# Attention value products: two rounded halves of V at full width, or plain float32 in two column halves

## The chip, the cores and the metric

One core of a Trainium2 chip runs the whole layer. The metric is the device time of one execution in microseconds (us). The kernel before takes 1442.31 us, the median of 3 runs (1439.19 to 1443.56).

## The reference, cut to what matters

The layer has two causal token mixers on the same 1024 tokens. NSA has eight heads in two groups, each with a compressed branch, a branch of selected blocks and a sliding window; DSA has eight heads over a latent. Both end in the same step: probabilities times values.

```python
# NSA, for a block of 128 tokens
o_cmp = jnp.einsum('ghtc,cgd->tghd', p_cmp, v_cmp)
o_slc = jnp.einsum('ghtk,gtkd->tghd', p, v_g)
o_win = jnp.einsum('ghtk,kgd->tghd', p, vw)
o = gates[..., 0:1] * o_cmp + gates[..., 1:2] * o_slc + gates[..., 2:3] * o_win
# DSA (heads, latent, values; shapes cut)
o_lat = jnp.einsum('htk,tkr->thr', p, c_g)
o_b = jnp.einsum('bthr,hrd->bthd', o_lat, w_uv)
```

A mixture of experts follows. All inputs are float32.

## The kernel before, in words

**The whole.** Most products on PE have operands of the type `F32R`, a rounded float32. The helper `split` makes two of them from one float32 operand: ACT casts the high part (line 59), DVE subtracts it from the source to get the low part (line 60), and products of high and low parts add up in PSUM. The stages are: projections (line 204) with the indexer of DSA and a search for its top keys on DVE (line 324), the attention of the 16 heads in the order of `ORDER`, the merge of the branches (line 711), the output projection and routing (line 978), and the experts (lines 1086 and 1109). Instructions are put in order on each engine by a planner that simulates the program; only the experts' order on PE is written out by hand.

**A head.** A head works on its 8 blocks of 128 queries in two halves of four (`gq`). Per query block, PE writes scores to a PSUM tile `s` (NSA: lines 573 and 574, compressed keys lines 580 and 581; DSA: lines 651 and 652, and 654 adds the selection mask). `softmax_part` adds the bias on DVE with a running extreme (line 482) and takes the exponential with its sum on ACT (line 484) into a tile `pb` or `pw`. POOL scales the rows by the reciprocal sums (`scale_rows`, line 465). Since all of the 16 blocks of 64 keys can be selected, the selected branch of NSA is causal attention over all keys.

**The value products.** The probabilities have queries on the partitions; the product needs keys there. `values` gets a list of runs: one key block with up to four query blocks that see it. It packs the runs into banks of at most four blocks (512 columns). Per bank, `transposed_pair` transposes up to four blocks on PE into a PSUM tile `pt` (line 490, three buffers) and splits it: ACT writes `pth`, DVE writes `ptl` (lines 59 and 60). Then PE takes, per run, a product with `pth` (line 545) and one with `ptl` (line 546). The stationary operand is a value block of 128 columns: the 64 columns of V's high part beside the 64 of its low part (`vv`, `vcc`, made at lines 163 and 164 and 420 and 421; `vb` for DSA, made by `dsa_values` at lines 626 and 627 from the products of line 622). So the output tile `pv` (one buffer) has the products with V's high part on partitions 0 to 63 and with its low part on 64 to 127, and `finish` adds the two halves, either through DRAM and POOL (line 514) or directly (lines 519 and 520).

**How many.** Over all heads there are 240 banks: 200 of 512 columns and 40 of 256.

Of the kernel before, what the change touches and what calls it, by code (L numbers as in the profile page):

```python
# [44 lines left out]
def layer_kernel(ctx: ExitStack, tc: tile.TileContext, A, out, dbg=None):  # L45
# [63 lines left out]
    ats = ExitStack()  # L109
    att = ats.enter_context(tc.tile_pool(name="att", bufs=1, side="right"))  # L110
    u0 = ctx.enter_context(tc.tile_pool(name="u0", bufs=1))
    vv = u0.tile([P, NT, 4, P], F32R, name="vv", tag="slot7")
    kch = att.tile([P, 2, 64], F32R, name="kch")
    kcl = att.tile([P, 2, 64], F32R, name="kcl")
    vcc = att.tile([P, 2, P], F32R, name="vcc")
    G.memset(f(vcc[0:64]), 0.0)
    cks = ExitStack()
    ckn = cks.enter_context(tc.tile_pool(name="ckp", bufs=1)).tile([P, NT, P], F32, name="ckn")
    cth = att.tile([P, T], F32R, name="cth")
# [17 lines left out]
    with tc.tile_pool(name="cr", bufs=1, side="right") as cr, tc.tile_pool(name="cr2", bufs=2, side="right") as cr2:  # L137
        big = [ps.tile([P, T], F32, name="s") for _ in range(3)]
        acc = [b[:, c] for b in big for c in HALF] + [ps.tile([P, 512], F32, name=n) for n in ("pt", "pv")]
        for k in range(KD):  # L140
            xw = cr2.tile([P, T + WN], F32, name="xw", bufs=4)
            nc.sync.dma_start(xw, A["xw"][k])
            xr, wr = xw[:, 0:T], xw[:, T:T + WN]
            split(xh[:, k], xl[:, k], xr)
            wh = cr2.tile([P, WN], F32R, name="wnh")
            wl = cr2.tile([P, WN], F32R, name="wnl")
            split(wh, wl, wr)
            for i in range(NT):
                ts = slice(i * P, (i + 1) * P)
                o = acc[i][:, :WN]  # L150
                PE.matmul(o, xh[:, k, ts], wh, start=(k == 0), stop=False)
                PE.matmul(o, xh[:, k, ts], wl, start=False, stop=False)
                PE.matmul(o, xl[:, k, ts], wh, start=False, stop=(k == KD - 1))
        nc.sync.dma_start(ident, A["ident"])
        V.tensor_copy(ident_b, ident)
        sq = cr.tile([P, NT], F32, name="sq")
        rstd = cr.tile([P, NT], F32, name="rstd")
        junk = cr.tile([P, P], F32, name="junk")
        gck = cr.tile([P, P], F32, name="gck")
        nc.sync.dma_start(gck, A["ckv_g"].partition_broadcast(P))  # L160
        for i in range(NT):
            src = acc[i][:, 0:256].rearrange("p (a d) -> p a d", a=4)
            S.copy(vv[:, i, :, 0:64], src)
            V.tensor_tensor(vv[:, i, :, 64:128], src, f(vv[:, i, :, 0:64]), op=ALU.subtract)
            S.activation(junk, acc[i][:, 280:408], AF.Square, accum_out=sq[:, i:i + 1])
            V.tensor_copy(ckn[:, i], acc[i][:, 280:408])
            V.tensor_copy(sig[:, i], acc[i][:, 256:280])
            V.tensor_scalar(wi[:, i], acc[i][:, 408:412], 0.5, None, op0=ALU.mult)  # L168
        V.tensor_scalar(sq, sq, 1.0 / 128, 1e-6, op0=ALU.mult, op1=ALU.add)
        G.tensor_tensor(rstd, sq, mhalf, op=ALU.pow)  # L170
        for i in range(NT):
            V.scalar_tensor_tensor(ckn[:, i], ckn[:, i], rstd[:, i:i + 1], gck, op0=ALU.mult, op1=ALU.mult)
# [212 lines left out]
    def compress(n, cp):  # L385
# [30 lines left out]
        if n == "kc":  # L416
            split(flat(kch), flat(kcl), t[:, 0:P])
        else:
            for g in range(2):
                S.copy(vcc[64:128, g, 0:64], t[g * 64:g * 64 + 64, 0:64])  # L420
                V.tensor_tensor(vcc[64:128, g, 64:128], t[g * 64:g * 64 + 64, 0:64], f(vcc[64:128, g, 0:64]),
                                op=ALU.subtract)

    with tc.tile_pool(name="cp", bufs=1, side="right") as cp, tc.tile_pool(name="bt", bufs=1, side="right") as bt:
        bias = bias_tables(bt)
# [64 lines left out]
            PE.transpose(t[:rows, x * P:(x + 1) * P], c, ident)  # L490
        return t[:rows, :n]

    def transposed_pair(cols, rows=P):
        t = transposed(cols, rows)
        n = P * len(cols)
        h = aw1.tile([P, 512], F32R, name="pth", bufs=3)
        l = aw1.tile([P, 512], F32R, name="ptl", bufs=3)
        split(h[:rows, :n], l[:rows, :n], t)
        return h[:rows, :n], l[:rows, :n]

    mc = aw0.tile([P, 8, 120], F32, name="mc")
    nc.sync.dma_start(mc, bass.AP(bc_d.tensor, bc_d.offset + 7, [[WP, P], [P * WP, 8], [1, 120]]))
# [21 lines left out]
            nc.sync.dma_start(od[n][h // 2][:, HALF[gq]], t)  # L524

    pair = {}

    def values(o, todo, gq, first, last):

        banks = []  # L530
        for run in sorted(todo, key=lambda r: -len(r[1])):
            for b in banks:
                if sum(len(r[1]) for r in b) + len(run[1]) <= 4:
                    b.append(run)
                    break
            else:
                banks.append([run])
        assert len(banks[0][0][1]) == 4
        for y, b in enumerate(banks):
            ph, pl = transposed_pair([c for r in b for c in r[1]])  # L540
            x = 0
            for z, (v, cols, i0) in enumerate(b):
                oo = o[:, (i0 - 4 * gq) * P:(i0 - 4 * gq + len(cols)) * P]
                n = slice(x, x + len(cols) * P)
                PE.matmul(oo, v, ph[:, n], start=first and y == 0, stop=False)  # L545
                PE.matmul(oo, v, pl[:, n], start=False, stop=last and y == len(banks) - 1 and z == len(b) - 1)  # L546
                x += len(cols) * P

    def nsa_head(h, kv, fin):
        g = h // 4  # L550
# [7 lines left out]
        for gq in range(2):  # L558
# [3 lines left out]
            for part in range(2):  # L562
                st = aw1.tile([P, 2, 8], F32, name="st", bufs=3)
                PR, PC, PS = {}, {}, {}
                for i in I4:
                    ts = slice(i * P, (i + 1) * P)
                    k0 = 0 if part == 0 else max(0, i - 4)
                    n = P * (i + 1 - k0)
                    kh, kl = (ksh, ksl) if part == 0 else (kwh, kwl)
                    s = ps.tile([P, T], F32, name="s")  # L570
                    for c in range(0, n, 512):
                        e = min(n, c + 512)
                        PE.matmul(s[:, c:e], q[:, ts], kh[:, k0 * P + c:k0 * P + e], start=True, stop=False)  # L573
                        PE.matmul(s[:, c:e], q[:, ts], kl[:, k0 * P + c:k0 * P + e], start=False, stop=True)  # L574
                    j = i % 4
                    if part == 0:
                        PR[i] = aw1.tile([P, T], F32, name="pb", bufs=8)[:, :n]
                        softmax_part(s[:, :n], m[:, T - n:T], PR[i], st, j)
                    else:
                        PE.matmul(s[:, 640:704], q[:, ts], kch[:, g], start=True, stop=False)  # L580
                        PE.matmul(s[:, 640:704], q[:, ts], kcl[:, g], start=False, stop=True)
                        pb = pwp.tile([P, 704], F32, name="pw", bufs=6)
                        PR[i], PC[i], PS[i] = pb[:, :n], pb[:, n:n + 64], pb[:, n - 64:n + 64]
                        softmax_part(s[:, :n], mw[:, 640 - n:640], PR[i], st, j)
                        softmax_part(s[:, 640:704], mc[:, h, 56 - 8 * i:120 - 8 * i], PC[i], st, 4 + j)
# [4 lines left out]
                if part:  # L590
                    V.tensor_tensor(st[:, 1, 4:8], st[:, 1, 4:8], sig[:, 4 * gq:4 * gq + 4, 3 * h], op=ALU.mult)
                for i in I4:
                    scale_rows(PR[i], st[:, 1, i % 4:i % 4 + 1])
                    if part:
                        scale_rows(PC[i], st[:, 1, 4 + i % 4:5 + i % 4])
                for k in range(4 * gq + 4):
                    ii = [i for i in I4 if i >= k and (part == 0 or i - 4 <= k)]
                    k0 = [0 if part == 0 else max(0, i - 4) for i in range(NT)]
                    todo.append((vv[:, k, 2 * part + g],
                                 [PR[i][:, (k - k0[i]) * P:(k - k0[i] + 1) * P] for i in ii], ii[0]))  # L600
# [17 lines left out]
    def dsa_values(h):  # L618
        s = ps.tile([P, T], F32, name="s")
        for i in range(NT):  # L620
            for c, w in ((cth, uvh), (cth, uvl), (ctl, uvh)):
                PE.matmul(s[:, i * P:(i + 1) * P], c[:, i * P:(i + 1) * P], w[:, h * 64:h * 64 + P],
                          start=(c is cth and w is uvh), stop=(c is ctl))
        vb = aw2.tile([P, NT, 2, P], F32R, name="vb", bufs=1)
        sv = s.rearrange("p (i j d) -> p i j d", i=NT, j=2)
        S.copy(vb[:, :, :, 0:64], sv)
        V.tensor_tensor(vb[:, :, :, 64:128], sv, f(vb[:, :, :, 0:64]), op=ALU.subtract)
        return vb

    def dsa_head(h, vb, fin):  # L630
# [10 lines left out]
        for gq in range(2):  # L641
# [3 lines left out]
            for i in I4:  # L645
# [3 lines left out]
                for c in range(0, n, 512):  # L649
# [2 lines left out]
                    PE.matmul(s[:, c:e], q[:, ts], kl[:, c:e], start=False, stop=i < 2)  # L652
                    if i >= 2:
                        PE.matmul(s[:, c:e], ident_b, selm[:, OFF[i] + c:OFF[i] + e], start=False, stop=True)
                PR[i] = aw1.tile([P, T], F32, name="pb", bufs=8)[:, :n]
                softmax_part(s[:, :n], m[:, T - n:T], PR[i], st, i % 4)
            V.tensor_scalar(st[:, 1], st[:, 1], 1e-30, None, op0=ALU.max)
            V.reciprocal(st[:, 1], st[:, 1])  # L658
            for i in I4:
                x = st[:, 1, i % 4:i % 4 + 1]  # L660
                if (i % 2 and h >= 6):
                    V.tensor_scalar(PR[i], PR[i], x, None, op0=ALU.mult)
                else:
                    scale_rows(PR[i], x)
            o = ps.tile([P, 512], F32, name="pv")
            todo = []
            for k in range(4 * gq + 4):
                ii = [i for i in I4 if i >= k]
                todo.append((vb[:, k, h % 2], [PR[i][:, k * P:(k + 1) * P] for i in ii], ii[0]))
            values(o, todo, gq, True, True)  # L670
            finish("b", h, gq, o, fin)
# [128 lines left out]

    RING = [5, 6, 7, 7, 17, 9, 10, 11, 12, 13, 14, 15, 16, 1, 2, 0]
    weights, loads = [], []
    sync = mybir.DependencyInfo(mybir.DependencyClass.Sync, mybir.DependencyReason.DATA)

    def prefetch(n=1):
        for _ in range(min(n, 3 * NE - len(weights))):
# [505 lines left out]
```

## Time and profile before

| what | value |
|---|---|
| timed runs | 1439.19, 1442.31, 1443.56 us |
| the profiled execution | 1442.7 us, its span 1440.9 us |
| PE busy | 1330.8 us, 92% of the span |
| PE weight loads busy | 1099.4 us, 76% |
| DVE busy | 1120.3 us, 78% |
| ACT busy | 764.8 us, 53% |
| POOL busy | 457.6 us, 32% |
| mean granted TensorE clock | 0.966 of full |

The page's busy time of PE counts each matmul up to a modelled end, and matmuls overlap in the pipeline, so a busy PE is not PE at its peak. Columns of the lists of groups: line, engine, operation, output tile and input tiles, partitions by elements and type, count, busy time in us and mean in ns, then the engine's idle time just before them and what ended it. PEld is the loading of weights.

### The profile page before, as it was taken

Reading aid. Unit: us, or ns where it says so; the run is one execution under the profiler, and the core shown is the slowest. Engines: PE = TensorE matmul, PEld = TensorE weight load, DVE = VectorE, ACT = ScalarE, POOL = GpSimd, SP = SyncE. Lnnn points to the kernel's source line nnn. Section 1 sums busy time; section 2 is a strip of 40 time slices with the busy share of each in tenths; the row PEclk is TensorE's granted clock in tenths of the full one; section 3 lists DMA queues with packets and bytes.
Section 4 is the critical chain, followed back from the end, with each engine's and each line's share of the span. In section 5 each row is a group of like instructions: output and inputs, shape, how many; then the busy total and the mean of one; then the engine's idle time right before and its main releaser. Section 6 shows DMA issues by size and latency. Waiting matters only on the chain.

```text
span 1440.9 us, 20097 instructions
## 1 busy us (share of the span) xinstructions
PE 1330.8 (92%) x6795; PEld 1099.4 (76%) x6795; DVE 1120.3 (78%) x2276; ACT 764.8 (53%) x1388; POOL 457.6 (32%) x457
## 2 busy tenths in 40 slices
PE   8999999999999999989999999999869999998950
PEld 8878888888887878878788778888757877776730
DVE  4323699889997878788889956654869999998946
ACT  4323323322117887778789732300248888877734
POOL 1112323312213344454444200002344444443315
PEclk9999999999998999999999999999979999999975
DMA  6023333497423332823521334765659999999834
GB/s 226 15 80 132 112 133 141 156 279 263 154 89 116 96 85 73 220 77 93 147 66 38 123 148 163 289 222 195 237 194 337 348 330 316 318 336 331 289 96 192
DMA packets 69476, 261.36 MB, mean 181 GB/s; under 512 B 15091, under 2 KB 16973, under 8 KB 57084
## 3 DMA queue, kind: packets, MB, share of 16 engines
q1 hardware_dynamic: 59644, 243.24, 48.9%
q0 software_dynamic: 9728, 16.82, 5.0%
q8 instruction: 54, 0.88, 0.3%
q14 instruction: 50, 0.41, 0.1%
HBM read 219.19 MB, written 70.70 MB: 201 GB/s over the span
## 4 chain that ended last, share of the span: by engine, by line
PE 60%; issue 16%; POOL 12%; DVE 5%; ACT 4%; DMA 2%; POOLq 0%; SPq 0%; DVEq 0%; ACTq 0%
PE s L204 24%; PE s L711 6%; PE s L978 6%; PE pt L490 5%; POOL acc_d L1114 5%; PE pv L546 3%; PE pv L545 3%; POOL xg L1046 2%; POOL xg L1043 2%; PE s L573 2%; PE pv L393 1%; PE s L574 1%; ACT pw L484 1%; PE s L652 1%; PE s L651 1%
## 5 line engine op out<-in xcount | busy, mean ns | idle before, releaser
L1086 PE MATMUL pt<-slot,slot 128*128 128x512 f32 x768 | 198.8, 405 | 11.9 <-DVE slot L1074 5.5
L1074 DVE TENSOR_TENSOR slot<-slot,slot 128x1024 fp32r<-128x1024 f32 x158 | 189.0, 1221 | 16.0 <-ACT slot L1073 10.0
L1073 ACT CAST slot<-slot 128x1024 fp32r<-128x1024 f32 x158 | 163.8, 1049 | 37.0 <-PE pt L1086 24.6
L1086 PEld LDWEIGHTS pt<-slot,slot 128*128 128x128 f32 x768 | 141.1, 190 | 51.6 <-DVE slot L1074 10.0
L186 POOL TENSOR_TENSOR wl<-wr,wh 128x1024 fp32r<-128x1024 f32 x39 | 95.0, 2438 | 262.0 <-ACT wh L185 262.0
L324 DVE TENSOR_SCALAR_CACHE_REDUCE jk<-idx,cand 128x384 bf16<-128x384 f32 (+1 forms) x186 | 164.4, 942 | 1.2
L60 DVE TENSOR_TENSOR ptl<-pt,pth 128x512 fp32r<-128x512 f32 (+1 forms) x240 | 148.3, 639 | 20.6 <-ACT pth L59 19.6
L59 ACT CAST pth<-pt 128x512 fp32r<-128x512 f32 (+1 forms) x240 | 128.5, 549 | 52.5 <-PE pt L490 44.3
L204 PE MATMUL s<-xh,wh 128*128 128x512 f32 x496 | 154.1, 391 | 2.3 <-DVE wi L168 1.4
L204 PE MATMUL s<-xh,wl 128*128 128x512 f32 x496 | 154.0, 390 | 0.0
L204 PE MATMUL s<-xl,wh 128*128 128x512 f32 x496 | 153.6, 389 | 0.0
L465 POOL TENSOR_SCALAR pb<-pb,st 128x128 f32<-128x128 f32 (+3 forms) x120 | 92.1, 786 | 183.4 <-DVE st L658 61.0
L185 ACT CAST wh<-wr 128x1024 fp32r<-128x1024 f32 x39 | 41.0, 1051 | 190.3 <-PE s L204 86.5
L1114 POOL DMA_INDIRECT acc_d<-wr,tkv x32 | 76.2, 2382 | 138.6 <-DVE wr L1113 138.6
L204 PEld LDWEIGHTS s<-xh,wh 128*128 128x128 f32 x496 | 92.2, 188 | 22.7 <-issue 2.6
L204 PEld LDWEIGHTS s<-xl,wh 128*128 128x128 f32 x496 | 93.1, 188 | 19.3
L204 PEld LDWEIGHTS s<-xh,wl 128*128 128x128 f32 x496 | 93.0, 188 | 19.2
L484 ACT ACTIVATE pb<-pb,st 128x128 f32<-128x128 f32 (+7 forms) x128 | 99.7, 780 | 12.0 <-DVE st L482 11.2
L1109 PE MATMUL s<-slot,hT 128*128 128x512 f32 x384 | 100.8, 408 | 2.0 <-DVE hT L60 1.5
L490 PE MATMUL pt<-ident,pb 128*128 128x128 f32 x576 | 92.7, 282 | 2.0 <-POOL pb L465 1.4
L978 PE MATMUL s<-slot,slot 128*128 128x512 f32 x384 | 93.3, 398 | 0.0
L1109 PEld LDWEIGHTS s<-slot,hT 128*128 128x128 f32 x384 | 70.5, 191 | 27.0 <-DVE hT L60 9.7
(345 smaller groups left out, 2932.5 us busy)
## 6 DMA issues: line engine op xcount, KB each, us to landing
slot<-in_w_ex_dram SPq DMA_DIRECT2D x79, 1024.0 KB
wr<-in_w_tt_dram SPq DMA_DIRECT2D x31, 512.0 KB
ring<-in_w_ex_dram SPq DMA_DIRECT2D x12, 1024.0 KB
b_d<-r_d SPq DMA_DIRECT2D x16, 576.0 KB
xw<-in_xw_dram SPq DMA_DIRECT2D x8, 718.0 KB
last<-in_w_ex_dram SPq DMA_DIRECT2D x5, 1024.0 KB
z_ga<-sh SPq DMA_DIRECT2D x8, 512.0 KB
slot<-b_d SPq DMA_DIRECT2D x8, 512.0 KB
```

Source lines behind the costliest of these rows:

```text
L59: S.copy(h, src)
L60: V.tensor_tensor(l, src, f(h), op=ALU.subtract)
L204: PE.matmul(z[:, c], w[:, k * P:(k + 1) * P], xx[:, k, c], start=(k == 0 and w is wh and xx is xh), stop=(k == KD - 1 and w is wl))
L324: V.tensor_scalar(jk[:, :n], idx[:, OFF[i]:OFF[i] + n], t, None, op0=op, op1=ALU.add, accum_out=cnt[:, i - 2:i - 1])
L484: S.activation(p, p, AF.Exp, bias=st[:, 0, j:j + 1], scale=-1.0, accum_out=st[:, 1, j:j + 1])
L490: PE.transpose(t[:rows, x * P:(x + 1) * P], c, ident)
L978: mm = PE.matmul(s[:, HALF[c]], MH[i // 2][a][:, k, (i % 2) * P:(i % 2) * P + P], WO[k][:, b, HALF[c]], start=(k == 0 and x == 0), stop=(k ...
L1073: S.copy(w[:, 0], self.w[k2 // 4][:, k2 % 4 // 2])
L1074: d = V.tensor_tensor(w[:, 1], self.w[k2 // 4][:, k2 % 4 // 2], f(w[:, 0]), op=ALU.subtract).ins
L1086: PE.matmul(self.a, self.xt[:, a, k * P:(k + 1) * P], w[:, b, (k - k2) * 512:(k - k2 + 1) * 512], start=(k == 0 and x == 0), stop=(k == KD ...
L1109: PE.matmul(s[:, c], self.hT[:, a, k * P:(k + 1) * P], w[:, b, c], start=(k == 0 and x == 0), stop=(k == 1 and x == 2))
L1114: d = G.indirect_dma_start(out=acc_d, out_offset=bass.IndirectOffsetOnAxis(ap=self.tok, axis=0), in_=y, in_offset=None, bounds_check=T - 1 ...
```

## The change

V is no longer split: `vv`, `vcc` and `vb` are float32 with 64 columns. The transposed probabilities are not split either: `flipped` makes one float32 copy of a bank, on ACT or on DVE. Banks are taken in pairs, called lanes here: the first bank's products write partitions 0 to 63 of `pv`, the second's 64 to 127, so that each product uses half of the array's columns. `finish` adds the two halves as before. If the number of banks is odd, the last one is divided into two; if a pair has at most four blocks in all, one transposition and one ACT copy serve both. The first product of a pair also waits for the pair's last copy. In a head's first half, key block 1 is given a zero block of probabilities for query block 0 (`score_tile` clears it on POOL), so that the first two banks both cover all four query blocks.

```diff
-    vv = u0.tile([P, NT, 4, P], F32R, name="vv", tag="slot7")
+    vv = u0.tile([P, NT, 4, 64], F32, name="vv", tag="slot7")
...
-    vcc = att.tile([P, 2, P], F32R, name="vcc")
-    G.memset(f(vcc[0:64]), 0.0)
+    vcc = att.tile([P, 2, 64], F32, name="vcc")
+    G.memset(vcc[0:64], 0.0)
...
-            S.copy(vv[:, i, :, 0:64], src)
-            V.tensor_tensor(vv[:, i, :, 64:128], src, f(vv[:, i, :, 0:64]), op=ALU.subtract)
+            S.copy(vv[:, i], src)
...
-    def transposed_pair(cols, rows=P):
-        t = transposed(cols, rows)
+    def flipped(cols, eng):
+        t = transposed(cols)
         n = P * len(cols)
-        h = aw1.tile([P, 512], F32R, name="pth", bufs=3)
-        l = aw1.tile([P, 512], F32R, name="ptl", bufs=3)
-        split(h[:rows, :n], l[:rows, :n], t)
-        return h[:rows, :n], l[:rows, :n]
+        h = aw1.tile([P, 512], F32, name="pth", bufs=6)
+        return h[:, :n], (S.copy if eng is S else V.tensor_copy)(h[:, :n], t).ins
...
-        assert len(banks[0][0][1]) == 4
-        for y, b in enumerate(banks):
-            ph, pl = transposed_pair([c for r in b for c in r[1]])
+        assert not first or all(len(banks[x][0][1]) == 4 for x in range(2))
+        if len(banks) % 2:
+            half = (sum(len(r[1]) for r in banks[-1]) + 1) // 2
+            ends = [[], []]
+            for v, cols, i0 in banks.pop():
+                a, b = cols[:half], cols[half:]
+                half -= len(a)
+                for x, (c, i) in enumerate(((a, i0), (b, i0 + len(a)))):
+                    if c:
+                        ends[x].append((v, c, i))
+            banks += ends
+        for y in range(0, len(banks), 2):
+            lanes, copies = [], []
+            short = sum(len(r[1]) for b in banks[y:y + 2] for r in b) <= 4
+            if short:
+                h, d = flipped([c for b in banks[y:y + 2] for r in b for c in r[1]], S)
+                copies.append(d)
             x = 0
-            for z, (v, cols, i0) in enumerate(b):
-                oo = o[:, (i0 - 4 * gq) * P:(i0 - 4 * gq + len(cols)) * P]
-                n = slice(x, x + len(cols) * P)
-                PE.matmul(oo, v, ph[:, n], start=first and y == 0, stop=False)
-                PE.matmul(oo, v, pl[:, n], start=False, stop=last and y == len(banks) - 1 and z == len(b) - 1)
-                x += len(cols) * P
+            for z in range(2):
+                if not short:
+                    h, d = flipped([c for r in banks[y + z] for c in r[1]], (S, V)[z])
+                    copies.append(d)
+                    x = 0
+                lane = []
+                for v, cols, i0 in banks[y + z]:
+                    lane.append((z, v, h[:, x:x + len(cols) * P], (i0 - 4 * gq) * P))
+                    x += len(cols) * P
+                lanes.append(lane)
+            steps = [lane[x] for x in range(max(map(len, lanes))) for lane in lanes if x < len(lane)]
+            for x, (z, v, m, c) in enumerate(steps):
+                end = last and y + 2 == len(banks) and not any(q[0] == z for q in steps[x + 1:])
+                d = PE.matmul(o[z * 64:z * 64 + 64, c:c + m.shape[1]], v, m,
+                              start=first and y == 0 and x < 2, stop=end).ins
+                if x == 0:
+                    tc.add_manual_dep(d, copies[-1].name, sync, reason="both halves together")
+
+    def score_tile(i):
+        p = aw1.tile([P, T], F32, name="pb", bufs=8)
+        if i == 0:
+            G.memset(p[:, P:2 * P], 0.0)
+        return p
...
-                    ii = [i for i in I4 if i >= k and (part == 0 or i - 4 <= k)]
+                    ii = [i for i in I4 if (i >= k or (i, k, part) == (0, 1, 0)) and (part == 0 or i - 4 <= k)]
...
-        vb = aw2.tile([P, NT, 2, P], F32R, name="vb", bufs=1)
-        sv = s.rearrange("p (i j d) -> p i j d", i=NT, j=2)
-        S.copy(vb[:, :, :, 0:64], sv)
-        V.tensor_tensor(vb[:, :, :, 64:128], sv, f(vb[:, :, :, 0:64]), op=ALU.subtract)
+        vb = aw2.tile([P, NT, 2, 64], F32, name="vb", bufs=2)
+        S.copy(vb, s.rearrange("p (i j d) -> p i j d", i=NT, j=2))
...
-                ii = [i for i in I4 if i >= k]
+                ii = [i for i in I4 if i >= k or (i, k) == (0, 1)]
```

## Rows read from the trace of the kernel before

**Rows 1.** The page: span, and PE's busy tenths in 40 slices of the span

```profile
span 1440.9 us, 20097 instructions
...
PE   8999999999999999989999999999869999998950
```

**Rows 2.** Busy time by stretch: the attention, 436 to 842 us

```profile
core 0: us, PE busy (x) PEld busy (x) DVE busy (x) ACT busy (x) POOL busy (x), PEclk, DMA share, GB/s
436.00:842.00 406.00, 389.14 (x2459) 330.68 (x2459) 342.29 (x939) 324.03 (x808) 164.15 (x253) 0.98 0.36 107
```

**Rows 3.** The chain of waits from 436 to 842 us, shares by line

```profile
by line: PE pt L490 17.8%; PE pv L546 10.8%; PE pv L545 9.9%; issue 5.4%; PE s L573 5.4%; PE s L574 4.9%; ACT pw L484 4.5%; PE s L652 4.2%; PE s L651 3.8%; PE s L654 3.6%; DVE ptl L60 3.6%; DVE pb L482 3.0%; PE s L711 2.6%; ACT pth L59 2.4%
```

**Rows 4.** Waits in the attention: us in total, times, longest us

```profile
ACT pth L59 <- PE pt L490: 44.3, 62, 3.5
DVE ptl L60 <- ACT pth L59: 19.6, 43, 1.4
PEld pv L546 <- DVE ptl L60: 6.6, 8, 2.4
PE pv L546 <- DVE ptl L60: 4.5, 4, 2.1
```

**Rows 5.** Line 545: matmuls, ns min/median/max, first and last start us, forms

```profile
L545 PE MATMUL pv<-pth,vv x192: 220/369/587, 448.2 to 806.7; 128*128 128x512 f32 x72, 128*128 128x384 f32 x40, 128*128 128x128 f32 x40, 128*128 128x256 f32 x40
...
L545 PE MATMUL pv<-pth,vb x96: 220/380/628, 484.3 to 841.0; 128*128 128x512 f32 x48, 128*128 128x384 f32 x16, 128*128 128x128 f32 x16, 128*128 128x256 f32 x16
...
L545 PE MATMUL pv<-pth,vcc x16: 392/477/526, 461.6 to 801.8; 128*128 128x512 f32 x16
```

**Rows 6.** A piece of the chain; then PE in order of time: start us, us

```profile
399.98 34.77 PE s L204 x154
...
950.62 3.64 PE L978 MATMUL s<-slot,slot 128*128 128x512 f32 x15
954.09 1.87 PE L955 MATMUL pt<-wrt,hT 128*128 128x36 f32 x16
955.80 1.07 PE L490 MATMUL pt<-ident,wr 128*128 128x128 f32 x8
```

**Rows 7.** Lines 922 (plain float32) and 580 (rounded): 64 columns, ns min/median/max

```profile
L922 PEld LDWEIGHTS pv<-val,at_place x32: 188/192/338, 984.5 to 1051.0; 128*128 128x128 f32 x32
L922 PE MATMUL pv<-val,at_place x32: 218/275/474, 984.7 to 1051.1; 128*128 128x64 f32 x32
...
L580 PE MATMUL s<-kch,slot x64: 192/245/362, 438.8 to 775.4; 128*128 128x64 f32 x64
```

**Rows 8.** The same view of PE's other lines in the attention: counts and forms

```profile
L490 PE MATMUL pt<-ident,pb x576: 270/272/475, 441.4 to 838.2; 128*128 128x128 f32 x192
...
L490 PE MATMUL pt<-ident,pw x304: 270/272/330, 453.8 to 802.6; 128*128 128x128 f32 x152
...
L573 PE MATMUL s<-slot,slot x192: 218/394/775, 436.1 to 775.2; 128*128 128x512 f32 x88, 128*128 128x128 f32 x56, 128*128 128x256 f32 x24, 128*128 128x384 f32 x24
...
L651 PE MATMUL s<-kbh,q x96: 222/422/589, 463.6 to 819.4; 128*128 128x512 f32 x48, 128*128 128x128 f32 x16, 128*128 128x256 f32 x16, 128*128 128x384 f32 x16
...
L654 PE MATMUL s<-selm,ident_b x80: 230/389/393, 467.5 to 820.0; 128*128 128x512 bf16 x48, 128*128 128x384 bf16 x16, 128*128 128x128 bf16 x8, 128*128 128x256 bf16 x8
```

**Rows 9.** Groups by form, ACT and DVE in the attention

```profile
L60 DVE TENSOR_TENSOR ptl<-pt,pth 128x512 fp32r<-128x512 f32 x200 | 133.2, 684 | 20.3 <-ACT pth L59 19.4
L59 ACT CAST pth<-pt 128x512 fp32r<-128x512 f32 x200 | 114.2, 584 | 50.8 <-PE pt L490 42.8 <-PE pv L545 5.6 <-DVE ptl L60 1.6
L60 DVE TENSOR_TENSOR ptl<-pt,pth 128x256 fp32r<-128x256 f32 x40 | 16.5, 413 | 0.3 <-ACT pth L59 0.2
L59 ACT CAST pth<-pt 128x256 fp32r<-128x256 f32 x40 | 15.0, 375 | 1.7 <-PE pt L490 1.6
L507 ACT COPY fin<-pv 128x512 f32<-128x512 f32 x20 | 11.6, 582 | 2.3 <-PE pv L546 2.3
L627 DVE TENSOR_TENSOR vb<-s,vb 128x1024 fp32r<-128x1024 f32 x4 | 4.9, 1220 | 2.6 <-ACT vb L626 2.6
```

**Rows 10.** Groups by form on POOL, whole program and attention

```profile
L1043 POOL MEMSET xg<- 128x1024 f32 x30 | 28.7, 956 | 49.7 <-PE s L1063 49.7
...
L465 POOL TENSOR_SCALAR pb<-pb,st 128x640 f32<-128x640 f32 x16 | 14.4, 898 | 102.9 <-DVE st L658 39.2 <-PE pv L546 15.1 <-ACT pth L59 14.1
```

More of the change, by code (lines that the diff above doesn't have):

```diff
@@ L419, in compress @@
             for g in range(2):
-                S.copy(vcc[64:128, g, 0:64], t[g * 64:g * 64 + 64, 0:64])
-                V.tensor_tensor(vcc[64:128, g, 64:128], t[g * 64:g * 64 + 64, 0:64], f(vcc[64:128, g, 0:64]),
-                                op=ALU.subtract)
+                S.copy(vcc[64:128, g], t[g * 64:g * 64 + 64, 0:64])
     with tc.tile_pool(name="cp", bufs=1, side="right") as cp, tc.tile_pool(name="bt", bufs=1, side="right") as bt:
@@ L526, in layer_kernel @@
     pair = {}
+    sync = mybir.DependencyInfo(mybir.DependencyClass.Sync, mybir.DependencyReason.DATA)
     def values(o, todo, gq, first, last):
@@ L576, in nsa_head @@
                     if part == 0:
-                        PR[i] = aw1.tile([P, T], F32, name="pb", bufs=8)[:, :n]
-                        softmax_part(s[:, :n], m[:, T - n:T], PR[i], st, j)
+                        PR[i] = score_tile(i)
+                        softmax_part(s[:, :n], m[:, T - n:T], PR[i][:, :n], st, j)
                     else:
@@ L592, in nsa_head @@
                 for i in I4:
-                    scale_rows(PR[i], st[:, 1, i % 4:i % 4 + 1])
+                    scale_rows(PR[i][:, :P * (i + 1 - (max(0, i - 4) if part else 0))], st[:, 1, i % 4:i % 4 + 1])
                     if part:
@@ L654, in dsa_head @@
                         PE.matmul(s[:, c:e], ident_b, selm[:, OFF[i] + c:OFF[i] + e], start=False, stop=True)
-                PR[i] = aw1.tile([P, T], F32, name="pb", bufs=8)[:, :n]
-                softmax_part(s[:, :n], m[:, T - n:T], PR[i], st, i % 4)
+                PR[i] = score_tile(i)
+                softmax_part(s[:, :n], m[:, T - n:T], PR[i][:, :n], st, i % 4)
             V.tensor_scalar(st[:, 1], st[:, 1], 1e-30, None, op0=ALU.max)
@@ L659, in dsa_head @@
             for i in I4:
-                x = st[:, 1, i % 4:i % 4 + 1]
+                x, p = st[:, 1, i % 4:i % 4 + 1], PR[i][:, :P * (i + 1)]
                 if (i % 2 and h >= 6):
-                    V.tensor_scalar(PR[i], PR[i], x, None, op0=ALU.mult)
+                    V.tensor_scalar(p, p, x, None, op0=ALU.mult)
                 else:
-                    scale_rows(PR[i], x)
+                    scale_rows(p, x)
             o = ps.tile([P, 512], F32, name="pv")
@@ L802, in layer_kernel @@
     weights, loads = [], []
-    sync = mybir.DependencyInfo(mybir.DependencyClass.Sync, mybir.DependencyReason.DATA)
     def prefetch(n=1):
```

## The prediction

> **What bounds the kernel now.** First the page's slices: TensorE is busy 80 to 99% of nearly every slice [rows 1], so I ask in which stage the change lies and what paces it there. The value products run from 448 to 841 us; the stage around them, the attention, is 436 to 842 us. The table by stretch gives PE 389, DVE 342 and ACT 324 of its 406 us, at nearly the full clock [rows 2]. The chain of that stretch goes through PE for most of its length, a fifth of it in the value products and about a sixth in the transposes [rows 3]. The waits show ACT waiting for transposes, DVE for ACT's half of the split, and PE for DVE's half, 11.1 us by name [rows 4]. So PE sets the end, with DVE and ACT close behind.
>
> PE's busy time overstates its work, since ends are modelled. Starts are better: 154 products of 512 columns take 34.77 us in the chain, 226 ns each, and eight transposes follow one another at about 110 ns (1.07 us less the last one's 0.27 gives 0.80 over seven steps) [rows 6]. I price 512 columns at 226, 384 at 170, 256 at 113 and 128 at 109 ns. The value products of one line are 136, 56, 56 and 56 of these [rows 5], and the other line has as many: 2 x (30.7 + 9.5 + 6.3 + 6.1) = 105 us. The stage's other work from the counts in [rows 8]: 880 transposes 96 us, NSA scores (L573, and L574 the same) 66, DSA scores (L651, L652 the same, L654) 50, and 128 compressed scores, 91 full-length and 96 short products in the rest, 45. Together 361 us. The stage lasts 406, so 45 us of it PE waits, or starts late.
>
> **What the change removes on ACT and DVE.** Before, each of 240 banks has an ACT copy and a DVE subtraction: ACT 114.2 + 15.0, DVE 133.2 + 16.5 us [rows 9]. Afterwards each bank has one copy, on ACT or on DVE. Packing the runs as the code does, an NSA head has 9 ACT copies of 512, one of 384, one of 256, and 8 DVE copies of 512 and one of 256; a DSA head has 4, 1, 1 on ACT and 4 of 512 on DVE. Over eight heads each: ACT 104 x 0.582 (L507 is such a copy) + 16 x 0.48 (between the forms) + 16 x 0.375 = 74 us, saving 55; DVE 96 x 0.684 + 8 x 0.413 = 69, if a copy costs what the subtraction does, saving 81, and L627's 4.9 [rows 9]. DVE falls to about 256 and ACT to 269 of 406 us. Neither is the bound, so this counts only through PE's 45 us of waiting. At least the named 11.1 us [rows 4] go; at most all 45. I take the middle, 28: what is left waits on score banks and softmax, which stay. The first stage loses eight subtractions of vv; a microsecond at most, and I count none.
>
> **What it does on PE.** Plain float32 is in the trace: L922 issues 16 products and has 32 records, each with its own weight load [rows 7]. So one product is two loads and two matmuls. How long one streams: the shortest 64-column matmul is 218 ns in plain float32 (L922) against 192 in the rounded type (L580) [rows 7]; 26 ns is what 64 columns take at 226 ns per 512 (28). So each record passes its columns twice, and a product four times. That rests on modelled ends and on 64 columns; L955's records, 106 ns apart [rows 6], would hide either, since no products with weights of 128 columns start closer together here. The bounds per product of 512 are then 452 ns (one pass per record) and 904 (two); I take 904.
>
> One block of 128 columns in one record is 113 ns; call that a unit. The blocks: an NSA head has 75 (one is the added zero block), a DSA head 37. The two lanes go to the two halves of the array. What a pair of lanes costs depends on how far the halves run at once, which no row shows; the three ways are the forecast and two rivals.
>
> In the forecast the halves run side by side, but records start in program order. Lane 0's product is issued whole before lane 1's: high 0, low 0, high 1, low 1. Low 0 needs high 0 out of its own half, and high 1 stands behind low 0, so high 1 runs beside low 0 and low 1 alone at the end: a pair of full banks takes three records, 12 units, where full overlap would take 8. Between pairs stand the next transposes, since a pair's copies have to be done first, so one pair rarely starts beside the last record of another. Counted so: an NSA head's first half has pairs of 12 + 5 units (selected) and 12 + 8 (window and compressed), its second 12 + 12 + 12 + 3 and 12 + 12 + 11: 111. A DSA head: 17 + 39 = 56. Eight of each: 1336 units, 151 us. Against 105 that is +46, and the 16 added transposes of zeros are 1.7 us.
>
> The Trainium skill, "TensorE: Matmul & The Clock Gate", part 3 under "What overlaps and what doesn't", says that matmuls keep program order in start and end; by that rule the three-record pair follows. No run here shows two halves at work.
>
> Unpriced on PE: a change between full and half array, twice for each of 136 pairs. In [rows 6] three kinds of product of the full array follow each other with no gap (each group starts before the last one's modelled end), so the lower end is nothing. At most each switch exposes a product's whole latency, 192 less 28 ns [rows 7]: 272 x 0.164 = 45 us. I take nothing, the nearer row, and keep the end for the range. The Trainium skill, "TensorEngine Tiling (Array Packing)", under "Key Properties", says that switching the tiling mode drains the engine; by it the 45 us would be nearer.
>
> **The rest.** POOL writes zeros into 128 columns of a tile for 16 half-heads, at most 0.96 us each (the row is for 1024 columns), 15 us in all; POOL idles over 100 us in one of its groups alone [rows 10], which hides it. It stands in front of the row scaling in POOL's order and waits for a free buffer of eight; if that cover failed, PE's transposes would be late by up to those 15 us, mostly in the first half-heads. The new wait of a pair's first product for the second copy holds PE's in-order queue, transposes and scores behind it, up to one copy, 0.68 us, for 136 pairs 93 us at worst; but before, the low product waited for ACT and DVE in turn, 1.27 us after its transposes, and lost 11 us, so it is in the 28. The second vb buffer lets the next DSA pair start early: nothing or a gain below the 4.9 us of L627.
>
> **The sum.** Against the profiled execution, 1442.7 us (span 1440.9; the median of the timed runs is 1442.3): 1442.7 + 46 + 2 - 28 = 1463. PE's work would then be 409 us, more than the stage now lasts, so no relief elsewhere makes this case faster. Its own range, relief 45 to 11 and switches 0 to half their bound: 1446 to 1502.
>
> **Rivals.**
> - Full overlap, faster. If a record for a busy half does not hold up the other half, or pairs follow each other directly, a pair takes 8 units: 39 block lengths per NSA head and 19 per DSA head, 58 x 8 x 2 = 928 units, 105 us, just what it is now. Then PE's work is unchanged and the 28 us of waiting go: 1442.7 + 2 - 28 = 1417 (1400 with all 45). For it: DVE and ACT lose a quarter and a sixth of their time, and the stage waits 45 us. Against it: lane order in the code, and pairs isolated by transposes. It decides as soon as more than about half of the third records overlap: then +23 meets -28. The Trainium skill, "TensorEngine Tiling (Array Packing)", under "Key Properties", says too that different tiles can load weights and multiply in parallel; by that sentence this rival would be the forecast.
> - The halves do not run at once (the change does not do what it says): (75 + 37) x 8 x 2 = 1792 units, 203 us, +98: 1442.7 + 98 + 2 - 28 = 1515. For it: no row shows any overlap. PE would be busy without a gap.
> - One pass per record: 668 units in the forecast's order, 75 us, -30: 1387. Against it the 26 ns of [rows 7].
> - The planner orders the whole program by its own costs, so other waits may move; a few microseconds either way round 1443.
>
> **Chances.** Records in order 0.40; full overlap 0.32; no overlap 0.18; one pass 0.04; planner noise about an unchanged time 0.06. The range reaches from full overlap with most of the waits gone to no overlap: 1402 to 1514. A difference of 0.3%, 4.3 us, can be told from none. Faster: 0.32 + 0.04 and a little of the noise, 0.37; same 0.08; slower 0.55.
>
> **What would show it.** In the changed trace each value product must have two records of 64 columns, 640 in all. If the forecast holds, in a pair the second lane's first record starts with the first lane's second, about 450 ns after the first, and the next transpose starts about 1.36 us after the pair began; with full overlap 0.9, with none 1.8. Stage 436 to 842 should grow by about 20 us, DVE fall to about 256, ACT to 269. It is wrong if the stage shrinks, if both lanes' first records start together, or if time moves outside this stage.

## The result and the profile after

The changed kernel takes 1463.0 us (median of 4 runs, 1460.86 to 1466.08) against 1442.55: ratio 1.0144, 95% interval 1.0128 to 1.0160, or 20.4 us slower. The forecast said 1463. Yet the 46 us that it added on PE and the 28 us that it took off for waiting did not come about as forecast, and a cost that it put at nothing did. These errors cancel, so the number was met by luck; the rest of this document is about that.

The page of the kernel after, its span and PE's slices:

```profile
span 1464.3 us, 19725 instructions
...
PE   8999999999999999999999999999969999998950
```

Busy time of the attention after, which now runs from about 438 to 864 us (columns as in [rows 2]):

```profile
438.00:864.00 426.00, 408.11 (x2493) 274.80 (x2507) 274.66 (x800) 282.14 (x705) 163.98 (x268) 0.99 0.34 102
```

The stretch is 20 us longer than in [rows 2]. DVE is busy 68 us less and ACT 42 less, and the stage is longer all the same. The loss is in this stage: from the first score product to the first output projection it took 436.1 to 924.5 us before and takes 438.5 to 946.5 now, 19.6 us more. The projection's row before, and then now (first and last starts stand behind the durations):

```profile
L978 PE MATMUL s<-slot,slot x384: 387/395/482, 924.5 to 1032.6; 128*128 128x512 f32 x192
```

```profile
L1004 PE MATMUL s<-slot,slot x384: 387/396/482, 946.5 to 1054.7; 128*128 128x512 f32 x192
```

The value products of the kernel after (line 566), to be read against [rows 5]:

```profile
L566 PE MATMUL pv<-pth,vv x400: 272/486/644, 450.3 to 819.2; 128*64 128x512 f32 x54, 128*64 128x128 f32 x36, 128*64 128x256 f32 x22, 128*64 128x384 f32 x22
...
L566 PE MATMUL pv<-pth,vb x208: 272/592/932, 487.1 to 862.8; 128*64 128x512 f32 x56, 128*64 128x128 f32 x32, 128*64 128x256 f32 x8, 128*64 128x384 f32 x8
...
L566 PE MATMUL pv<-pth,vcc x32: 592/618/643, 459.0 to 816.4; 128*64 128x512 f32 x32
```

640 records of 64 columns, two for each of 320 products. PE in order of time, two pairs of lanes (start us, us, what):

```profile
561.85 0.34 PE L681 MATMUL s<-selm,ident_b 128*128 128x384 bf16 x1
562.12 0.64 PE L566 MATMUL pv<-pth,vcc 128*64 128x512 f32 x1
562.13 0.86 PE L566 MATMUL pv<-pth,vv 128*64 128x384 f32 x2
562.60 0.59 PE L566 MATMUL pv<-pth,vcc 128*64 128x512 f32 x1
562.82 0.38 PE L566 MATMUL pv<-pth,vv 128*64 128x128 f32 x2
563.13 0.66 PE L487 MATMUL pt<-ident,pb 128*128 128x128 f32 x4
...
567.28 0.28 PE L603 MATMUL s<-slot,slot 128*128 128x256 f32 x1
567.65 1.08 PE L566 MATMUL pv<-pth,vb 128*64 128x512 f32 x4
568.66 0.44 PE L602 MATMUL s<-slot,slot 128*128 128x384 f32 x1
```

In the first pair, the compressed branch's lane starts at 562.12 and the other at 562.13. Neither waits for the other's second record. The first lane's second record follows at 562.60, 0.48 us after the first: 512 columns, passed twice. The second pair, two full banks, holds PE for 1.01 us from its start to the next score product; two passes of two records side by side are 0.90, records in program order would be 1.36. So the halves run fully side by side.

But each stretch of such products (half-array products with nothing else between them) has a gap on both sides. The product before the first pair streams 384 columns, 0.17 us from 561.85, and the pair starts 0.10 us after that. The second pair starts 0.26 us after the 256 columns before it have streamed; by the 0.90 us it streams until 568.55, and the next product starts 0.11 us later. Counted over all records the trace has 119 such stretches, not 136, since some pairs follow one another directly. By the prediction's prices for streaming, the median gap is 0.09 us before a stretch and 0.11 behind it, 24 us for 119. The same count in the kernel before gives 0.004 and 0.010 us around the products of line 545.

The loader of weights shows the same (groups by form, attention, kernel after; the last column is the idle time just before them):

```profile
L487 PEld LDWEIGHTS pt<-ident,pb 128*128 128x128 f32 x592 | 65.5, 142 | 47.1 <-issue 29.1 <-POOL pb L462 11.2 <-ACT pth L494 2.6
...
L566 PEld LDWEIGHTS pv<-pth,vv 128*64 128x64 f32 x400 | 28.5, 135 | 26.7 <-issue 19.8 <-ACT pth L494 1.8 <-DVE st L479 0.9
```

The loader stood idle, waiting for nothing in the profile ("issue"), for 29.1 us before the transposes of `pb`, and 19.8 before the products with `vv`. In the kernel before it stood idle for 0.4 us on "issue" in the same group of transposes: loads ran ahead of the matmuls. Around the half-array products they don't.

```profile
L490 PEld LDWEIGHTS pt<-ident,pb 128*128 128x128 f32 x576 | 70.2, 144 | 12.2 <-POOL pb L465 2.1 <-DVE ptl L60 1.4 <-issue 0.4
```

The copies cost what was estimated:

```profile
L494 ACT COPY pth<-pt 128x512 f32<-128x512 f32 x104 | 59.4, 583 | 39.4 <-PE pt L487 38.7
...
L494 DVE COPY pth<-pt 128x512 f32<-128x512 f32 x96 | 66.0, 687 | 45.2 <-PE pt L487 44.9
```

### The profile page after: what moved, and what is told of

Its sections match the earlier page's. It is cut to its first block, busy times and chain, and to the rows that moved or that the text cites. A ratio compares the mean times of both kernels' runs of the same rounds, so it can differ in the third digit from the quotient of the medians.

```text
span 1464.3 us, 19725 instructions
## 1 busy us (share of the span) xinstructions
PE 1357.2 (93%) x6829; PEld 1050.5 (72%) x6843; DVE 1047.5 (72%) x2126; ACT 722.1 (49%) x1284; POOL 455.7 (31%) x473
## 4 chain that ended last, share of the span: by engine, by line
PE 65%; issue 16%; POOL 11%; DMA 2%; DVE 2%; ACT 2%; POOLq 0%; SPq 0%; DVEq 0%; ACTq 0%
PE s L203 23%; PE pt L487 7%; PE pv L566 7%; PE s L1004 6%; PE s L738 6%; POOL acc_d L1140 5%; POOL xg L1072 2%; PE s L602 2%; POOL xg L1069 2%; PE s L603 2%; PE pv L392 1%; PE s L678 1%; PE s L679 1%; PE pt L981 1%; PE s L681 1%
## 5 line engine op out<-in xcount | busy, mean ns | idle before, releaser
L1112 PE MATMUL pt<-slot,slot 128*128 128x512 f32 x768 | 202.6, 411 | 11.0 <-ACT slot L1099 5.6
L1112 PEld LDWEIGHTS pt<-slot,slot 128*128 128x128 f32 x768 | 144.6, 195 | 50.4 <-ACT slot L1099 7.4
L203 PEld LDWEIGHTS s<-xl,wh 128*128 128x128 f32 x496 | 94.0, 190 | 19.8
L203 PEld LDWEIGHTS s<-xh,wl 128*128 128x128 f32 x496 | 93.8, 189 | 19.6
L494 DVE COPY pth<-pt 128x512 f32<-128x512 f32 (+1 forms) x104 | 69.4, 667 | 48.7 <-PE pt L487 48.5
L487 PEld LDWEIGHTS pt<-ident,pb 128*128 128x128 f32 x592 | 65.5, 142 | 47.1 <-issue 29.1
L494 ACT COPY pth<-pt 128x512 f32<-128x512 f32 (+2 forms) x136 | 71.9, 546 | 53.4 <-PE pt L487 52.7
```

Of the source, the lines that this page charges most:

```text
L203: PE.matmul(z[:, c], w[:, k * P:(k + 1) * P], xx[:, k, c], start=(k == 0 and w is wh and xx is xh), stop=(k == KD - 1 and w is wl))
L494: return h[:, :n], (S.copy if eng is S else V.tensor_copy)(h[:, :n], t).ins
L1112: PE.matmul(self.a, self.xt[:, a, k * P:(k + 1) * P], w[:, b, (k - k2) * 512:(k - k2 + 1) * 512], start=(k == 0 and x == 0), stop=(k == KD ...
```

## The experiments

Three questions were open: what the relief of ACT and DVE was worth, what a stretch of half-array products costs beside its streaming, and whether the added wait or the products themselves were the loss.

**1. The relief by itself, in the kernel before.**

```diff
-        l = aw1.tile([P, 512], F32R, name="ptl", bufs=3)
-        split(h[:rows, :n], l[:rows, :n], t)
-        return h[:rows, :n], l[:rows, :n]
+        turn[0] += 1
+        (S.copy if turn[0] % 2 else V.tensor_copy)(h[:rows, :n], t)
+        return h[:rows, :n], h[:rows, :n]
```

(`pth` gets six buffers.)

> The kernel before, with one copy per bank, on ACT and DVE in turn, in place of cast and subtraction; both products of a run read this one copy (the low part of the probabilities is left out, the high part is counted twice). PE's instructions are those of before, so this is the relief of ACT and DVE by itself. If the relief is worth what the prediction took, 28 us of PE's 45 us of waiting: about 1414 us. If, as the trace after suggests, PE is paced by its own work and most waits stay: 1430 to 1442 us.

Measured: 1486.66 us against 1443.26 (ratio 1.0303, 1.0284 to 1.0322). The whole time can't be read here: with other values the routing differs, and line 1088 of the experts does 792 products where the kernel before does 768. So only what lies ahead of the routing counts. The first group is scores, the second output projection, the third experts:

```profile
L575 PE MATMUL s<-slot,slot x192: 218/393/775, 437.1 to 781.9; 128*128 128x512 f32 x88, 128*128 128x128 f32 x56, 128*128 128x256 f32 x24, 128*128 128x384 f32 x24
...
L980 PE MATMUL s<-slot,slot x384: 387/395/482, 929.6 to 1037.8; 128*128 128x512 f32 x192
...
L1088 PE MATMUL pt<-slot,slot x792: 388/396/795, 1065.4 to 1427.8; 128*128 128x512 f32 x198
```

From the first score to the output projection 492.5 us, where before had 488.4. The busy time says that the relief was there:

```profile
437.00:848.00 411.00, 390.17 (x2444) 331.74 (x2459) 285.53 (x820) 273.29 (x689) 162.83 (x253) 0.97 0.36 106
```

DVE 57 us and ACT 51 us less than in [rows 2], and no gain at all; the granted clock was 0.97 where it was 0.98 before. The waiting moved. The planner orders the program anew for every kernel here, and PE, which waited 4.5 us for `ptl` before [rows 4], now waits longer for POOL's scaled rows and for score banks. The kernel before, and then this one:

```profile
PE s L573 <- DVE st L482: 1.9, 6, 0.5
...
PE pt L490 <- POOL pb L465: 1.4, 2, 1.0
```

```profile
PE s L575 <- DVE st L482: 5.9, 13, 1.4
PE pt L490 <- POOL pb L465: 5.6, 6, 2.0
```

**2. The old work on ACT and DVE, put back into the changed kernel.**

```diff
-        h = aw1.tile([P, 512], F32, name="pth", bufs=6)
-        return h[:, :n], (S.copy if eng is S else V.tensor_copy)(h[:, :n], t).ins
+        h = aw1.tile([P, 512], F32, name="pth", bufs=3)
+        d = S.copy(h[:, :n], t).ins
+        l = aw1.tile([P, 512], F32, name="ptl", bufs=3)
+        V.tensor_tensor(l[:, :n], t, h[:, :n], op=ALU.subtract)
+        return h[:, :n], d
```

> The changed kernel with the old work on ACT and DVE put back: ACT copies every bank, DVE subtracts every bank into a tile that nobody reads (three buffers each, as before). PE's instructions are those of the changed kernel. If the relief of ACT and DVE was worth 28 us, they are lost: about 1491 us. If it was worth the 0 to 9 us that the waits show: 1463 to 1472 us.

Measured: 1459.8 us (ratio 1.0104, 1.0083 to 1.0126). Busy time of its attention:

```profile
437.00:862.00 425.00, 409.99 (x2491) 274.32 (x2507) 340.44 (x936) 328.92 (x809) 164.02 (x268) 0.99 0.35 103
```

DVE is back at 340 us and ACT at 329, and the kernel is no slower than the changed one; the intervals put it a little ahead. From both sides, then: that work on ACT and DVE was worth nothing to PE on balance, once the planner had ordered the rest anew. Both theories expected a loss or none, not a gain of 3 us. In this trace PE waits 1.2 us for POOL's scaled rows where the changed kernel waits 7.8, and 3.7 us for ACT's copies where that waits 2.1. Whether this makes the gain is not shown.

**3. Halves in one.**

```diff
-                d = PE.matmul(o[z * 64:z * 64 + 64, c:c + m.shape[1]], v, m,
+                w = 0 if y else z * 64
+                d = PE.matmul(o[w:w + 64, c:c + m.shape[1]], v, m,
```

(The end of an accumulation moves with it.)

> The changed kernel, with both lanes of every pair but the first of each part in the same half of the array (partitions 0 to 63 of the output; the sum is the same). If the halves run fully side by side in the changed kernel, 20 blocks per NSA head and 10 per DSA head now run one after another: 240 x 0.226 = 54 us more, about 1517 us. If records ran in the order of the forecast, a third of the pair's time was already alone, and half as much is lost: about 1490 us. If the halves never overlapped: 1463 us.

Measured: 1512.79 us (ratio 1.0475, 1.0454 to 1.0496), 50 us over the changed kernel. That is full overlap's number, within 5 us, and not the forecast's.

**4. Without the pair's wait.**

```diff
-                if x == 0:
-                    tc.add_manual_dep(d, copies[-1].name, sync, reason="both halves together")
```

> The changed kernel without the first product's added wait for the pair's last copy. If the wait costs PE time: up to 10 us faster, about 1453 us. If the loss is in the switches of the array: no difference beyond 3 us, or slower where another instruction now comes between the two lanes and adds a switch.

Measured: 1522.84 us (ratio 1.0542, 1.0523 to 1.0561): 60 us slower than the changed kernel, far outside what either theory expected. PE in order of time shows why:

```profile
574.19 1.07 PE L566 MATMUL pv<-pth,vv 128*64 128x512 f32 x2
575.20 0.65 PE L487 MATMUL pt<-ident,pw 128*128 128x128 f32 x4
575.78 1.07 PE L566 MATMUL pv<-pth,vv 128*64 128x512 f32 x2
576.78 0.66 PE L487 MATMUL pt<-ident,pw 128*128 128x128 f32 x4
```

Now a lane's two records go out as soon as its own copy is there, the planner puts four transposes in between, and the other lane runs alone: 1.0 us for one bank, where a pair took 1.0 for two. The trace has 171 stretches in place of 119. In this planner's order the wait is what makes the overlap.

**5. Two pairs behind one another.**

```diff
-        for y in range(0, len(banks), 2):
+        for y0 in range(0, len(banks), 2 * GROUP):
+            got = [(y, *lanes_of(y)) for y in range(y0, min(len(banks), y0 + 2 * GROUP), 2)]
...
-                    tc.add_manual_dep(d, copies[-1].name, sync, reason="both halves together")
+                    if x == 0 and y == y0:
+                        tc.add_manual_dep(d, got[-1][2].name, sync, reason="both halves together")
```

(`GROUP` is 2; `lanes_of` holds the old loop body up to the products.)

> The changed kernel, with the products of two pairs issued behind one another once the copies of both are there: 72 stretches of half-array products in place of 136, the same products and copies. If each change between full and half array costs about 0.1 us, as the gaps in the trace after suggest: 64 stretches fewer at 0.2 us, 13 us faster than the changed kernel, about 1450 us. If the loss lies elsewhere (products themselves, or the wait for copies): 1463 us, or slower, since the first product now waits for four copies.

Measured: 1467.0 us (ratio 1.0157, 1.0131 to 1.0183), no gain over the changed kernel. The trace has 72 stretches against 119, so 47 fewer and not the 64 of the expectation; even these did not pay. Busy time in four pieces of this kernel, and of its whole attention:

```profile
618.00:622.00 4.00, 2.75 (x15) 1.63 (x12) 2.63 (x7) 2.86 (x9) 1.79 (x1) 1.00 1.02 228
622.00:628.00 6.00, 4.51 (x19) 4.31 (x20) 4.12 (x19) 3.50 (x14) 4.33 (x5) 0.50 0.46 180
720.00:727.00 7.00, 4.44 (x24) 2.66 (x23) 5.36 (x18) 4.38 (x12) 3.83 (x3) 1.00 0.92 252
727.00:731.00 4.00, 4.00 (x18) 3.61 (x18) 3.11 (x15) 3.22 (x15) 3.82 (x7) 0.60 0.75 240
...
436.00:865.00 429.00, 406.36 (x2492) 288.08 (x2507) 272.52 (x800) 282.75 (x705) 165.66 (x268) 0.96 0.35 102
```

PE was busy for 2.75 of 4 us and 4.44 of 7, and then the granted clock was 0.50 and 0.60 of full, that is partly or wholly the 1.2 GHz level. Over the attention it is 0.96, against 0.99 in the changed kernel. As a rough estimate, if all of the attention went with the clock, it would last 412 and 422 us at full clock (429 x 0.96, 426 x 0.99): about ten us saved, near the 9 that 47 stretches at 0.2 us give, and as much given back. No run here separates what the clock took from what waiting took.

**6. A short pair joined to the one before it.** The same edit with groups of one pair, plus a following short pair.

> The changed kernel with a short pair's products issued straight behind those of the pair before it: 104 stretches of half-array products in place of 136, and only one more copy to wait for in the joined ones. By the switches' price of 0.26 us: 8 us faster than the changed kernel, about 1455 us. If waiting takes it back, as with two pairs each: 1463 us or slower.

Measured: 1469.52 us (ratio 1.0179, 1.0156 to 1.0201), no gain, and by the medians 6.5 us slower than the changed kernel, though the intervals just overlap. The planner left 107 stretches of the 119, 12 fewer and not 32, so some 2 us and not 8 were to be had. Waits for ACT's copies grew: PE and its loader stood idle before the value products until `pth` from ACT for 7.5 us, against 3.0. The rest is not explained.

**7. The price of a stretch, measured by itself in the kernel before.** Four kernels add one small product of zeros per bank, 240 in all, that differ only in its columns and type:

```diff
+                if z == 0:
+                    PE.matmul(o[0:64, 0:64], zero[:, 0:64], f(ph)[:, 0:64], start=False, stop=False)
                 PE.matmul(oo, v, pl[:, n], start=False, ...
```

This is the one in plain float32 with 64 columns; the others have 128, or the rounded type (`zero` in F32R and `ph` as it is).

> The kernel before, with one more product per bank between its high and its low product: 64 columns of moving data against a stationary tile of 64 zero columns, into partitions 0 to 63 of the output (it adds zeros). 240 stretches of one half-array product. If a stretch costs 0.26 us for entering and leaving, as the trace after shows, beside 0.03 of streaming: about 70 us more, 1512 us. If changing costs nothing: 240 x 0.06 = 14 us more, 1457 us.

> As e5_half_switch, but the stationary tile has 128 zero columns and the output is all 128 partitions, so the array stays whole. Each costs what a product with 128 columns of weights takes, 0.109 us: 240 x 0.109 = 26 us more, 1469 us, less what falls into waits. The difference between the two kernels is the price of the switches: 44 us if a stretch costs 0.26 us, below nothing if switching is free.

> As e5_half_switch, but the added product of 64 zero columns is in plain float32 (two records), like the value products of the changed kernel; the moving data are the same bits read as plain float32. If plain float32 in half an array costs 0.26 us a stretch for entering and leaving, beside two loads of 64 columns: 240 x 0.32 = 77 us of PE work, of which some 13 us fall into waits as in e6_full_zero, so about 1507 us. If the half array as such is free, as e5_half_switch had it: 240 x 0.11 = 26 us less 13, about 1457 us.

> As e9_half_plain with 128 zero columns: plain float32 in the whole array, two records of 0.109 us each. 240 x 0.218 = 52 us, less some 13 that fall into waits: about 1483 us. If the price of a stretch belongs to plain float32 and not to the half array, this kernel has it too: 1483 + 62 = 1545 us, slower than e9_half_plain.

| added product | us | before | ratio, 95% interval | added us |
|---|---|---|---|---|
| rounded, 64 columns | 1458.79 | 1443.9 | 1.0100, 1.0079 to 1.0120 | 14.9 |
| rounded, 128 columns | 1459.47 | 1443.9 | 1.0118, 1.0093 to 1.0142 | 15.6 |
| plain, 64 columns | 1526.89 | 1442.86 | 1.0583, 1.0562 to 1.0604 | 84.0 |
| plain, 128 columns | 1479.27 | 1442.86 | 1.0257, 1.0233 to 1.0281 | 36.4 |

Half the columns in the rounded type have no price that can be told from noise: 14.9 against 15.6 us. Plain float32 in the whole array costs 36.4 us with its two records for each product, near the 40 expected for two records and nothing else. The two together have a price: plain float32 in half the array costs 84.0 - 36.4 = 47.6 us more than in the whole, 0.198 us for each of 240 stretches. By itself, this kernel came out 20 us above the nearer of its two expected numbers, 1507; what makes these 20 is not shown. The loader's rows, of the plain product with 64 columns, the plain one with 128, and the rounded one with 64, in this order:

```profile
L549 PEld LDWEIGHTS pv<-pth,zero 128*64 128x64 f32 x480 | 45.8, 134 | 61.5 <-issue 56.0
```

```profile
L549 PEld LDWEIGHTS pv<-pth,zero 128*128 128x128 f32 x480 | 86.8, 189 | 9.7
```

```profile
L549 PEld LDWEIGHTS pv<-pth,zero 128*64 128x64 f32 x240 | 33.2, 139 | 3.8
```

Only the first waits on "issue", 56.0 us. A stretch of it in order of time, PE:

```profile
562.49 0.40 PE L547 MATMUL pv<-pth,vv 128*128 128x512 f32 x1
562.82 0.33 PE L549 MATMUL pv<-pth,zero 128*64 128x64 f32 x2
563.07 0.66 PE L490 MATMUL pt<-ident,pb 128*128 128x128 f32 x4
```

The 512 columns stream for 0.226 us, until 562.72; the small product starts 0.10 us later.

## Why the prediction was right, and where it was wrong

- **PE sets the end: right**, more strictly than I used it. Taking work off ACT and DVE gave nothing (experiments 1 and 2), also where the waits of before named their tiles. DVE fell to 275 us and ACT to 282, not to 256 and 269.
- **Two records per product, two passes per record: right.** 640 records; 0.48 us between a lane's first and second record of 512 columns. One reading beside it was wrong: products with 128 columns of weights do start closer together than 106 ns in the kernel before. Lines 580 and 581, rounded, with 64 columns, start 0.03 us apart (565.97 and 566.00).
- **Records in program order, +46 us: wrong.** "High 1 stands behind low 0" did not happen: first records start 0.01 us apart, which the prediction named as a sign of being wrong. A full pair takes 1.01 us, and putting both lanes into one half costs 50 us. This was the rival of full overlap: 928 units, 105 us, no change in streaming. The rule of the Trainium skill, "TensorE: Matmul & The Clock Gate", "What overlaps and what doesn't", says that matmuls keep program order in start and end, and gave me the in-order time; this trace differs from it, with lane 1's first record at 562.13 before lane 0's second at 562.60, though the code has lane 0's product first. The trace lists records by their start and not by their issue, so the order of issue is the code's. The trace decides.
- **Switches at nothing: wrong.** I took the lower end from products of the whole array; measured, a stretch costs 0.198 us (experiment 7), so the 119 of the trace 24 us, or 27 for 136. The upper end, 45 us, held. The Trainium skill, "TensorEngine Tiling (Array Packing)", "Key Properties", says that a change of the tiling mode drains the engine; the gaps of 0.10 us on both sides agree with it. I quoted that sentence and gave it no weight in the sum.
- **Relief of 28 us: wrong.** Two experiments put it near nothing. From the sum, 24 for the stretches and 1.7 for the added transposes make 26 where 20.4 were measured, so some 6 us are left over. It may be the low product's wait for DVE's half, 11.1 us in [rows 4], of which the changed kernel keeps 3.7 us of waiting for `pth`. Experiment 1 took that wait away too and gained nothing, at a granted clock of 0.97, with other waits in its place. This remains open.
- **POOL's zeros "hidden": the writes were cheap, the cover is open.** They take 0.20 us each, 3.3 in all, not up to 0.96 and 15. But PE's waits for POOL's scaled rows grew from 2.1 to 7.8 us (7.4 of them for `pb`, against 1.4), the one by name that grew most. In experiment 2, with the same writes, PE waits 1.2 us for them. So the writes alone do not make the wait, and what makes it is not shown.

```profile
PE pt L487 <- POOL pb L462: 7.4, 10, 1.7
```

- **The sum.** Forecast 46 + 2 - 28 = 20; found 24 + 2 - 6 = 20, the 6 being what is left over and not measured by itself. Both the size and the direction were luck. PE's work grew, as forecast, but through the gaps that were put at nothing and not through the order of records. With the right overlap and my own other terms I would have said 1417, a gain.
- **The new wait**, which I counted within the 28, costs little: PE and its loader stood idle before the value products for 3.7 us until a copy. It is the condition for the overlap: without it the kernel loses 60 us.

No experiment pointed to a version faster than the kernel before; the best one with half-array products, experiment 2, stays 1% behind it.

## What to carry to other kernels

Before halving the array for plain float32, count the stretches: with two passes per record and two records, the streaming of two halves side by side only equals that of rounded high and low products at full width, and each stretch costs 0.2 us on top, its way in and out together. If two lanes are to overlap, tie them together in the order of the engine that runs them. And when one engine paces a stage, price the relief of the others at nothing until an experiment that removes their work alone says otherwise. A forecast that comes out right to the microsecond can still be wrong in each large term, so compare the terms and not only the total.

## What was not expected of the hardware

- Products in the two column halves ran side by side to within 0.01 us at the start, with both records of each lane (1.01 us for a pair, gaps included, against 1.0 us for a lane alone).
- 64 columns of weights in the rounded type showed none of the stretch's price: the loader stood idle for 3.8 us over 240 loads, while the same in plain float32 stopped it for 56 us over 480.
- Saving stretches at the price of thinner PE work (2.75 busy of 4 us) went with stretches at the 1.2 GHz level (granted clock 0.50), and the saving was gone; that the clock took it is likely, and not separated from waiting.
